# A second seven-block product pair in six attention heads, with the softmax's row copies and scaling on ScalarE

## The chip, the core and the metric

The kernel runs on one core of a Trainium2 chip. The metric is the device time of one execution in microseconds (us). The engines are named as the profile names them: PE (TensorE; PEld its weight loads), DVE (VectorE), ACT (ScalarE), POOL (GpSimd) and SP (SyncE, which here issues most DMAs).

## The reference

A trunk of two pre-norm residual layers over 512 tokens of width 1024: layer 0 mixes with dilated attention, layer 1 with a Mamba-2 scan, each is followed by a gated ConvFFN, and a last RMSNorm ends it. The change lies in the attention of layer 0, which has three groups (dilations 1, 4 and 16) of eight heads of width 128:

```python
def dilated_attention_mixer(h, w_qkv, w_o, cos, sin):
    qkv = (h @ w_qkv).reshape(bsz, s, N_ATTN_GROUPS, 3, ATTN_HEADS_PER_GROUP, ATTN_HEAD_DIM)
    q = apply_partial_rope(qkv[:, :, :, 0], cos, sin)
    k = apply_partial_rope(qkv[:, :, :, 1], cos, sin)
    v = qkv[:, :, :, 2].astype(jnp.float32)
    for g in range(N_ATTN_GROUPS):
        dil = ATTN_DILATIONS[g]
        o_g, lse_g = dilated_window_attention(q[:, :, g], k[:, :, g], v[:, :, g], dil,
                                              ATTN_WINDOWS[g] // dil)
        outs.append(o_g)
        lses.append(lse_g)
    wts = jax.nn.softmax(jnp.stack(lses, axis=2), axis=2)
    o = jnp.einsum("bsgh,bsghe->bshe", wts, jnp.stack(outs, axis=2))
    return o.reshape(bsz, s, ATTN_OUT_WIDTH).astype(h.dtype) @ w_o
```

Rope turns the first 32 of a head's 128 channels. Each group has its own softmax, and the three are merged by the softmax of their log sums.

## The kernel before

**Products.** An fp32 product is made of three matmuls: every operand is split into a high part (a cast to fp32r, on ACT, L127 or L328) and a low part (operand minus high part, on DVE, L128 or L331), and `mm3` issues high by high, high by low and low by high (`long_product`, L136). A plain product of one weight unit (1024 rows in eight steps, 128 columns, all 512 tokens) is 24 matmuls of 512 columns.

**Product pairs.** The query and the key of one group and head may be made together as a `Pair`: the two 128-column outputs, halved by tokens, and the halved input form a product of 2x2 blocks that is made with seven block products in place of eight. A block is 12 matmuls of 256 columns, so a pair is 84 of these in place of 48 of 512. It loads four pieces of weights (a, b, c and q; q's tile has two buffers), makes four sums of them on DVE (`sums`, L317, L318, L320, L321), splits the four results a, b, c, d (`split`), runs the blocks 0 to 6 (`block`; 0 and 1 use a, 2 and 3 use b, 4 and 5 use c, 6 uses d), and combines their PSUM banks: `query` (DVE, L525, L527), `key` (DVE, L532 to L534), with the rope's swap of rows (`swap`, a shuffle on DVE, L541, and a product on POOL, L542) and `turn` (DVE L547, POOL L548). ACT copies block 0's and 1's banks to a kept tile (L518) and block 4's bank out (L520). `QK_PAIRS` lists the pairs: group 1 of heads 0 to 6. All other queries and keys are plain products, read by `qk_read` (DVE L465, shuffle L468, POOL L469 and L470). Of v, group 0 is made per head (`v0_step`: product, scaled copy tv on DVE, L555; then `v0_turn` transposes it on PE to pv, L562); the values of groups 1 and 2 are made in two halves for all heads, the second of them in the stage of head 4 (`late_values`).

**A head's attention.** `attend(h)` is a generator, and each `next(core)` runs one step: scores of the first two and the last two blocks of 128 queries (PE L640 to L642 for groups 0, 1, 2; DVE masks and takes the row maximum, L646, L650; ACT takes the exponentials, L652), `spread` (17 small copies that bring a row's maxima and sums from other partitions, L659, L662), `join` (the merge of the groups, DVE L668 to L676, with an exponential on ACT, L671), `weigh` (rows times their share, L683), transposes of the rows (`by_key`, PE L690, ACT L692) and values (PE L698, L703; ACT L731, DVE L732).

**What sets the order.** The projections of head h+1 are woven into the attention of head h: `attend_and_project` for h = 0 to 5, `attend_and_fetch` for h = 6. A stage is called here after the head whose projections it makes, so "the stage of head 2" is `attend_and_project(1)`. Inside `tc.manual_schedule` PE, DVE and ACT run in the order in which the code stands; SP's and POOL's orders are the scheduler's. The stage of head 2 goes from 130.70 to 175.80 us in the profile. PSUM has three banks for products, three auxiliary ones and two for scores; raw weights have four buffers and split weights five.

Of the kernel before, what the change touches and what calls it, by code (L numbers as in the profile page):

```python
# [29 lines left out]
EPS = 1e-5  # L30
NEG = -1e30
FF_PARTS = ((0, 8), (8, 8), (16, 6))
QK_PAIRS = ((0, 1), (1, 1), (2, 1), (3, 1), (4, 1), (5, 1), (6, 1))
STORED = 6


# [17 lines left out]
def trunk(ctx: ExitStack, tc: tile.TileContext, A, out):  # L54
# [48 lines left out]
    rbc = cp.tile([P, S], F32, tag="rbc", name="rbc")  # L103

    cp.tile([P, 8], F32, tag="gap", name="gap")
    k2.tile([P, 24], F32, tag="gap2", name="gap2", bufs=1)
    nc.scalar.dma_start(par[:, :C_FFN], A["par"][:, :C_FFN])
    V.memset(ones, 1.0)
    V.memset(mhalf, -0.5)
# [280 lines left out]
    for k, xp in enumerate(xps):  # L390
        square(k, xp, ssum, V)
    load2, second = v_steps(2, 0)
    minus = sm.tile([P, KD], F32, tag="minus", name="minus", bufs=1)
    V.tensor_scalar(minus, par[:, C_MIX : C_MIX + KD], -1.0, None, op0=ALU.mult)
    combined = []

# [169 lines left out]
    def qk_steps(h):  # L566
        return [
            lambda cut=None, g=g, c=c: qk_step(h, g, c, cut) for g in range(NG) for c in range(2)
        ] + [lambda: v0_step(h)]

    E = mybir.EngineType
    WRITTEN = {E.PE, E.DVE, E.Activation}

    with tc.manual_schedule(engines=WRITTEN):
        load2(1)
        V.tensor_tensor(cr, cr, rbc, op=ALU.mult)
        second[0]()
        combine(1)
        load2(2)
        V.tensor_tensor(sr[0:ROPE, :], sr[0:ROPE, :], rbc[0:ROPE, :], op=ALU.mult)  # L580
        second[1]()
        combine(2)
        load2(3)
        second[2]()
        combine(3)
        ready(0, 0, 0)
        one = Pair(0, 1)
        second[3]()
        one.sums()
        one.split("ab")  # L590
        p = qk_products(0, 0, 0)
        qk_read(0, 0, 0, p)
        one.split("cd")
        ready(0, 2, 0)
        for i in range(3):
            one.block(i)
        one.query(0)
        for i in range(3, 6):
            one.block(i)
        one.query(1)  # L600
        ready(0, 2, 1)
        one.block(6)
        one.turn(0)
        one.key()
        p = qk_products(0, 2, 0)
        ready(0, 0, 1)
        qk_read(0, 2, 0, p)
        p = qk_products(0, 2, 1)
        ready_v0(0)
        qk_read(0, 2, 1, p)  # L610
        p = qk_products(0, 0, 1)
        qk_read(0, 0, 1, p)
        ready(1, 0, 0)
        v0_step(0)
        ready(1, 0, 1)

    scale = HD ** -0.5
    oh, ol = [], []
# [1 line left out]
    def attend(h):  # L620
# [14 lines left out]
        def scores(i0):  # L635
            for i in (i0, i0 + 1):
                sc = side_bank("sc")
                ii = slice(i * P, (i + 1) * P)
                k0 = P if i == 0 else 0
                T.matmul(sc[:, k0:256], q[0][:, ii], kk[0][:, i * P - P + k0 : (i + 1) * P], start=True, stop=True)  # L640
                T.matmul(sc[:, 256:384], q[1][:, ii], kk[1][:, ii], start=True, stop=True)
                T.matmul(sc[:, 384:512], q[2][:, ii], kk[2][:, ii], start=True, stop=True)  # L642
                pr = t2("pr", "pr", 7, s3)
                prs[i] = pr
                for w, cs in enumerate((slice(k0, 256), slice(256, 512))):
                    V.tensor_tensor_reduce(  # L646
                        out=pr[:, cs], in0=sc[:, cs], in1=mask[:, cs], scale=1.0, scalar=NEG * 2,
                        op0=ALU.add, op1=ALU.max, accum_out=own[:, w, 0, i : i + 1],
                    )
                V.tensor_scalar(neg[:, :, i], own[:, 0:2, 0, i], -scale, None, op0=ALU.mult)  # L650
                for w, cs in enumerate((slice(k0, 256), slice(256, 512))):
                    SC.activation(  # L652
                        pr[:, cs], pr[:, cs], AF.Exp, bias=neg[:, w, i : i + 1], scale=scale,
                        accum_out=own[:, w, 1, i : i + 1],
                    )

        def spread():

            V.tensor_copy(own[:, 2], own[:, 0])  # L659
            for a in range(4):  # L660
                for b in range(4):
                    V.tensor_copy(oth[32 * b : 32 * b + 32, :, :, a], own[32 * a : 32 * a + 32, 1:3, :, b])  # L662

        def join():

# [13 lines left out]
        def weigh(i):  # L679
            k0 = P if i == 0 else 0  # L680
            pr = prs[i]
            for w, cs in enumerate((slice(k0, 256), slice(256, 512))):
                V.tensor_scalar(pr[:, cs], pr[:, cs], share[:, w, i : i + 1], None, op0=ALU.mult)  # L683

        def by_key(i):
            k0 = P if i == 0 else 0
# [20 lines left out]

        scores(0)
        yield
        scores(2)  # L710
        yield
        spread()
        yield
# [63 lines left out]

    def together(core):

        for n in (1, 1, 2, 2, 1, 1):  # L780
            for _ in range(n):
                next(core, None)
            yield

    def attend_and_project(h, after=()):

        core, m = attend(h), h + 1
        follow = lambda c: ready(m + 1, 0, c)
        with tc.manual_schedule(engines=WRITTEN):
            pair = Pair(m, 1)  # L790
            next(core)
            pair.sums((0,))
            v0_turn(h)
            pair.split("a")
            pair.sums((1,))
            p = qk_products(m, 0, 0)
            qk_read(m, 0, 0, p)
            pair.split("bc")
            ready(m, 2, 0)
            p = qk_products(m, 0, 1)  # L800
            qk_read(m, 0, 1, p)
            next(core)
            for i in range(3):
                pair.block(i)
            pair.query(0)
            pair.split("d")
            ready(m, 2, 1)
            for i in range(3, 5):
                pair.block(i)
            next(core)  # L810
            pair.block(5)
            pair.query(1)
            next(core)
            next(core)
            pair.block(6)
            ready_v0(m)
            pair.turn(0)
            pair.key()
            p = qk_products(m, 2, 0)
            qk_read(m, 2, 0, p)  # L820

            p = qk_products(m, 2, 1, cut=(5, lambda: next(core)))
            next(core)
            qk_read(m, 2, 1, p)
            for f in after[:2] or (lambda: follow(0), lambda: follow(1)):
                f()
            v0_step(m)
            next(core, None)
# [3 lines left out]
    def late_values():  # L832

        (l1, s1), (l2, s2) = v_steps(1, 1), v_steps(2, 1)
        loads = [lambda l=l, u=u: l(u) for l in (l1, l2) for u in range(4)]
        loads += [lambda c=c: ready(5, 0, c) for c in range(2)]
        steps = s1 + s2
        out = loads[:2]
        for i, f in enumerate(steps):
            if i + 2 < len(loads):  # L840
                out.append(loads[i + 2])
            out.append(f)
        return out

    def attend_and_fetch(h):

# [8 lines left out]

        with tc.manual_schedule(engines=WRITTEN):
            next(core)
            v0_turn(h)
            ready(m, 1, 0)
            products(0, 0)  # L860
# [2 lines left out]
            products(0, 1)  # L863
            ready(m, 1, 1)
            read(0, 1)
            next(core)
            products(1, 0)
            ready(m, 2, 0)
# [6 lines left out]
            read(1, 1)  # L875
            products(2, 0, cut=(5, lambda: next(core)))
            next(core)
            fetch_heads(1)
            read(2, 0)
            products(2, 1)  # L880
            fetch_heads(2)
            read(2, 1)
            next(core, None)

    for h in range(NH):
# [892 lines left out]
```

## Time and profile before

| | |
|---|---|
| time, median of 3 runs | 1611.13 us (1610.71 to 1611.44) |
| the profiled execution | 1610.11 us, of which its span 1608.0 us |
| busy share of the span | PE 99%, PEld 87%, DVE 77%, ACT 45%, POOL 35% |
| attention of layer 0 | about 48 to 470 us of the span |

The span goes from the first instruction to the last; the execution's own time is 2.1 us longer. Rows of a timeline give start, duration (both us), engine, line of the kernel, operation, output <- inputs with buffer numbers left out, shapes, a count where like instructions are put together, and in brackets how long the engine had stood idle and what ended that. POOL's steps have their duration from being started to being done, so that a step that stands by while another instruction goes on shows a long duration.

### The profile page before, as it was taken

The page shows a single profiled execution, that of the slowest core. Times are in us where ns is not written, and L with a number is a line of the kernel's source. Part 1 is how long each engine was busy: PE and PEld are TensorE (multiplying, and loading weights), DVE is VectorE, ACT ScalarE, POOL GpSimd, SP SyncE. Part 2 cuts the span into 40 slices and gives each one's busy share as a digit, 9 for nine tenths or more (in the row PEclk, how much of TensorE's full clock was granted, in tenths as well). Part 3 has the DMA queues.
Part 4 walks back from the last instruction along what each step waited for, and adds up shares of the span by engine and source line. Part 5 has one row for each costly group of instructions (what it writes and reads, how often), then busy time and mean ns, then how long its engine had stood idle before and what let it go on. Part 6 is the DMA issues. An engine that isn't in the chain of part 4 may idle for free.

```text
span 1608.0 us, 23435 instructions
## 1 busy us (share of the span) xinstructions
PE 1598.8 (99%) x8864; PEld 1398.7 (87%) x8864; DVE 1230.4 (77%) x2083; ACT 720.1 (45%) x1132; POOL 570.6 (35%) x432
## 2 busy tenths in 40 slices
PE   9999999999999999999999999999999999999998
PEld 8889988899888889889888888888888888988987
DVE  7788886388757868778757899978898687867864
ACT  6434332333435543544445455544443454444443
POOL 0434453045412753652331222222112285365230
PEclk9999999999999999999999999999999999999999
DMA  6322323123334323423333433323332322332341
GB/s 222 105 93 92 99 86 118 54 72 105 123 107 131 102 69 92 151 64 101 128 99 109 149 108 115 104 98 123 121 128 74 109 73 81 110 125 73 96 127 53
DMA packets 61600, 168.44 MB, mean 105 GB/s; under 512 B 7152, under 2 KB 10608, under 8 KB 61488
## 3 DMA queue, kind: packets, MB, share of 16 engines
q1 hardware_dynamic: 60928, 166.42, 32.1%
q8 instruction: 70, 1.15, 0.3%
q10 hardware_dynamic: 560, 0.53, 0.1%
q14 instruction: 42, 0.34, 0.1%
HBM read 163.19 MB, written 3.74 MB: 104 GB/s over the span
## 4 chain that ended last, share of the span: by engine, by line
PE 85%; DVE 4%; POOL 1%; issue 1%; ACT 0%; DVEq 0%; POOLq 0%; ACTq 0%
PE u L136 29%; PE qk L136 7%; PE xs L136 5%; PE wso L136 5%; PE z L136 5%; PE v L136 4%; PE b L136 3%; PE c L136 3%; PE wo L136 3%; PE wd L136 2%; PE wz L136 2%; PE py L1351 1%; PE pf L1359 1%; PE pst L1306 1%; PE qk41r L136 1%
## 5 line engine op out<-in xcount | busy, mean ns | idle before, releaser
L136 PE MATMUL u<-xh,hi_u 128*128 128x512 f32 x704 | 269.8, 383 | 0.0
L136 PE MATMUL u<-xh,lo_u 128*128 128x512 f32 x704 | 269.4, 383 | 0.0
L136 PE MATMUL u<-xl,hi_u 128*128 128x512 f32 x704 | 267.3, 380 | 0.0
L136 PEld LDWEIGHTS u<-xh,lo_u 128*128 128x128 f32 x704 | 131.7, 187 | 25.1
L128 DVE TENSOR_TENSOR lo_u<-raw_u,hi_u 128x1024 fp32r<-128x1024 f32 x88 | 123.6, 1414 | 38.9 <-ACT hi_u L127 38.9
L136 PEld LDWEIGHTS u<-xl,hi_u 128*128 128x128 f32 x704 | 131.7, 187 | 24.6
L136 PEld LDWEIGHTS u<-xh,hi_u 128*128 128x128 f32 x704 | 131.7, 187 | 22.4 <-issue 0.4
L127 ACT CAST hi_u<-raw_u 128x1024 fp32r<-128x1024 f32 x88 | 91.8, 1047 | 107.5 <-PE u L136 62.3
L469 POOL TENSOR_TENSOR rotqk<-rotqk,sr 32x512 f32<-32x512 f32 x34 | 74.4, 2188 | 157.6 <-DVE rotqk L468 157.6
L920 DVE SCALAR_TENSOR_TENSOR au<-u,par,au 128x511 f32<-128x511 f32 (+1 forms) x152 | 113.3, 746 | 20.4 <-ACT au L918 18.0
L945 POOL TENSOR_TENSOR au<-au,au 128x512 f32<-128x512 f32 x43 | 58.0, 1349 | 170.7 <-DVE au L920 156.9
L136 PE MATMUL qk<-xh,hi_qk 128*128 128x512 f32 x272 | 105.5, 388 | 0.0
L136 PE MATMUL qk<-xh,lo_qk 128*128 128x512 f32 x272 | 104.2, 383 | 0.0
L1296 POOL TENSOR_TENSOR xdd<-xdt,dec 128x384 f32<-128x384 f32 x16 | 18.0, 1139 | 241.0 <-DVE xdt L1295 241.0
L933 DVE TENSOR_TENSOR u<-u,rbc 128x512 f32<-128x512 f32 x76 | 52.8, 695 | 66.2 <-PE u L136 65.9
L136 PE MATMUL qk<-xl,hi_qk 128*128 128x512 f32 x272 | 103.4, 380 | 0.0
L918 ACT ACTIVATE au<-u,par 128x512 f32<-128x512 f32 x76 | 59.1, 778 | 22.8 <-DVE u L933 21.2
L652 ACT ACTIVATE pr<-pr,neg 128x256 f32<-128x256 f32 (+1 forms) x64 | 31.1, 487 | 76.7 <-DVE neg L650 76.3
L1096 POOL TENSOR_TENSOR xr<-xr,sums 128x512 f32<-128x512 f32 x16 | 33.1, 2069 | 82.1 <-DVE sums L1094 82.1
L239 POOL TENSOR_TENSOR ssum<-ssum,sq 128x512 f32<-128x512 f32 x21 | 32.5, 1549 | 83.2 <-ACT sq L238 82.8
L136 PEld LDWEIGHTS qk<-xh,lo_qk 128*128 128x128 f32 x272 | 50.9, 187 | 9.6
L136 PEld LDWEIGHTS qk<-xl,hi_qk 128*128 128x128 f32 x272 | 51.0, 187 | 8.8
(3304 smaller groups left out, 4773.5 us busy)
## 6 DMA issues: line engine op xcount, KB each, us to landing
raw_u<-in_wup SPq DMA_DIRECT2D x88, 512.0 KB, 3.4
raw_qk<-in_wqk SPq DMA_DIRECT2D x34, 512.0 KB, 3.4
raw_xs<-in_win SPq DMA_DIRECT2D x16, 512.0 KB, 3.3
raw_z<-in_win SPq DMA_DIRECT2D x16, 512.0 KB, 3.6
lm<-rows SPq DMA_DIRECT2D x32, 256.0 KB, 5.2
raw_wso<-in_wso SPq DMA_DIRECT2D x16, 512.0 KB, 3.3
raw_v<-in_wv SPq DMA_DIRECT2D x12, 512.0 KB, 4.4
raw_wd<-in_wdn SPq DMA_DIRECT2D x16, 384.0 KB, 3.4
```

Of the source, the lines that this page charges most:

```text
L127: SC.copy(hi[:, s], raw[:, s])
L128: low.tensor_tensor(lo[:, s], raw[:, s], hi.bitcast(F32)[:, s], op=ALU.subtract)
L136: T.matmul(in_turns(dst), w, in_turns(x), start=first, stop=last, skip_group_check=skip)
L239: add.tensor_tensor(ssum, ssum, sq, op=ALU.add)
L469: G.tensor_tensor(rot[R, :], rot[R, :], sr[R, :], op=ALU.mult)
L652: SC.activation(pr[:, cs], pr[:, cs], AF.Exp, bias=neg[:, w, i : i + 1], scale=scale, accum_out=own[:, w, 1, i : i + 1],)
L918: latest["tap"] = SC.activation(dst, src, AF.Identity, bias=col(c_b), scale=col(c_w + taps - 1))
L920: V.scalar_tensor_tensor(dst[:, j:], src[:, : S - j], col(c_w + taps - 1 - j), dst[:, j:], op0=ALU.mult, op1=ALU.add,)
L933: V.tensor_tensor(dst, p, rbc, op=ALU.mult)
L945: by.tensor_tensor(ab[1], ab[0], ab[1], op=ALU.mult)
L1096: G.tensor_tensor(low3, low3, v.unsqueeze(1).to_broadcast([P, 2, 256]), op=ALU.add)
L1296: G.tensor_tensor(v4(u[:, 0:384], 3), v4(t[:, 0:384], 3), b3(dec3[:, 0:3, heads[x]], 64), op=ALU.mult)
```

## The change

Heads 1 to 6 get a second pair, for group 2. In a stage the blocks of the two pairs now come first (`one` for group 1, `two` for group 2), and group 0's two plain products and v0 last. The first pair of the next head is begun at the end of a stage (`next_pair`: sums, splits of a and b, splits of c and d), ahead of the scores of the next stage; `late_values` does that for head 5. The exponentials become a step of their own (`powers`). The copies of `spread` and the products of `weigh` go from DVE to ACT. `attend_and_fetch` reads group 2's products before it fetches stored heads. The tile `minus` gets the place of a filler tile.

```diff
-QK_PAIRS = ((0, 1), (1, 1), (2, 1), (3, 1), (4, 1), (5, 1), (6, 1))
+QK_PAIRS = ((0, 1),) + tuple((h, g) for h in range(1, 7) for g in (1, 2))
...
-    k2.tile([P, 24], F32, tag="gap2", name="gap2", bufs=1)
+    minus = k2.tile([P, 24], F32, tag="gap2", name="minus", bufs=1)[:, :KD]
...
+    begun_pair = {}
+
+    def next_pair(h):
+
+        if h == NH - 1:
+            ready(h, 0, 0)
+            yield
+            ready(h, 0, 1)
+            yield
+        else:
+            pair = begun_pair[h] = Pair(h, 1)
+            pair.sums()
+            yield
+            pair.split("ab")
+            yield
+            pair.split("cd")
+        yield
...
-        ready(1, 0, 0)
+        following = next_pair(1)
+        next(following)
+        next(following)
         v0_step(0)
-        ready(1, 0, 1)
+        next(following)
...
         def spread():
 
-            V.tensor_copy(own[:, 2], own[:, 0])
+            SC.copy(own[:, 2], own[:, 0])
             for a in range(4):
                 for b in range(4):
-                    V.tensor_copy(oth[32 * b : 32 * b + 32, :, :, a], own[32 * a : 32 * a + 32, 1:3, :, b])
+                    SC.copy(oth[32 * b : 32 * b + 32, :, :, a], own[32 * a : 32 * a + 32, 1:3, :, b])
...
-                V.tensor_scalar(pr[:, cs], pr[:, cs], share[:, w, i : i + 1], None, op0=ALU.mult)
+                SC.activation(pr[:, cs], pr[:, cs], AF.Copy, scale=share[:, w, i : i + 1])
...
     def attend_and_project(h, after=()):
 
         core, m = attend(h), h + 1
-        follow = lambda c: ready(m + 1, 0, c)
+        follow = next_pair(m + 1)
         with tc.manual_schedule(engines=WRITTEN):
-            pair = Pair(m, 1)
+            one, two = begun_pair.pop(m), Pair(m, 2)
             next(core)
-            pair.sums((0,))
+            next(core)
             v0_turn(h)
...
+            two.sums()
+            one.block(0)
+            one.block(1)
+            two.split("a")
+            one.block(2)
+            one.query(0)
+            two.split("b")
+            for i in range(3, 6):
+                one.block(i)
+            one.query(1)
+            one.block(6)
+            one.turn(0)
+            one.key()
+            next(core)
+            two.split("c")
+            two.block(0)
+            two.block(1)
+            next(core)
+            two.block(2)
+            two.query(0)
+            two.split("d")
+            ready(m, 0, 0)
+            for i in range(3, 6):
+                two.block(i)
+            two.query(1)
+            ready(m, 0, 1)
+            next(core)
+            two.turn(0)
+            next(core)
+            next(core)
+            two.block(6)
+            two.key()
             p = qk_products(m, 0, 0)
             qk_read(m, 0, 0, p)
+            ready_v0(m)
+            if not after:
+                next(follow)
+            p = qk_products(m, 0, 1, cut=(6, lambda: next(core)))
+            next(core)
             qk_read(m, 0, 1, p)
...
+            for f in after[:2] or (lambda: next(follow),) * 2:
                 f()
             v0_step(m)
             next(core, None)
...
     def attend_and_fetch(h):
...
             products(2, 0, cut=(5, lambda: next(core)))
             next(core)
+            read(2, 0)
             fetch_heads(1)
-            read(2, 0)
             products(2, 1)
+            read(2, 1)
             fetch_heads(2)
-            read(2, 1)
```

The lines of the changed kernel are other ones: its scores' reductions are L665 and L669, the pair's steps L524 to L546, the plain readings L464 and L467, tv L554, `spread` L683 and L686, `weigh` L707. In the rows below a name has the head, the group and 0 for a query or 1 for a key at its end (qk201: head 2, group 0, key; v02: the values of head 2), and a buffer's number.

DVE in the stage of head 2, around the second pair of score reductions. Before:

```order
L331 TENSOR_TENSOR lob_qk21_1430<-rawb_qk21_1353,hib_qk21_1429 128x1024
L331 TENSOR_TENSOR loc_qk21_1434<-rawc_qk21_1354,hic_qk21_1433 128x1024
L128 TENSOR_TENSOR lo_qk220_1439<-raw_qk220_1437,hi_qk220_1438 128x1024
L465 TENSOR_TENSOR qk201_1468<-qk201_1443,cr_368 128x4x4x32
L468 STREAM_SHUFFLE rotqk201_1470<-qk201_1443 32x512
L646 ISA pr_1478,own_1360<-sc_1474,mask_372 128x256
```

And with the change, at the same place:

```order
L526 TENSOR_TENSOR qk210_1477<-qk210_1477,qk21r3_1473 128x256
L540 STREAM_SHUFFLE rotqk210_1564<-qk210_1477 32x512
L546 TENSOR_TENSOR qk210_1477<-qk210_1477,cr_367 128x512
L531 TENSOR_TENSOR qk211_1478<-keptqk21_1476,qk21r2_1474 128x256
L532 TENSOR_TENSOR qk211_1478<-qk211_1478,keptqk21_1476 128x256
L533 TENSOR_TENSOR qk211_1478<-qk211_1478,qk21r4_1475 128x256
L540 STREAM_SHUFFLE rotqk211_1584<-qk211_1478 32x512
L546 TENSOR_TENSOR qk211_1478<-qk211_1478,cr_367 128x512
L665 ISA pr_1593,own_1438<-sc_1589,mask_371 128x256
L669 TENSOR_SCALAR neg_1440<-own_1438 128x2
L331 TENSOR_TENSOR loc_qk22_1606<-rawc_qk22_1432,hic_qk22_1605 128x1024
L524 TENSOR_TENSOR qk220_1614<-keptqk22_1613,qk22r2_1611 128x256
```

Before, the split of c (loc) stood ahead of the reductions and well ahead of its blocks; now the first pair's combining and the reductions stand ahead of the second pair's loc.

DVE at the end of the same stage, up to tv02. Before:

```order
L468 STREAM_SHUFFLE rotqk221_1748<-qk221_1685 32x512
L128 TENSOR_TENSOR lo_qk300_1754<-raw_qk300_1752,hi_qk300_1753 128x1024
L128 TENSOR_TENSOR lo_qk301_1760<-raw_qk301_1758,hi_qk301_1759 128x1024
L555 TENSOR_TENSOR tv02_1789<-v02_1764,rbc_99 128x4x4x32
L732 TENSOR_TENSOR o1_1799<-o1_1799,po1_1723 128x4x4x32
```

And with the change:

```order
L317 TENSOR_TENSOR rawa_qk31_1810<-q_qk31_1813,rawb_qk31_1811 128x512
L318 TENSOR_TENSOR rawb_qk31_1811<-rawa_qk31_1810 128x512
L320 TENSOR_TENSOR rawc_qk31_1812<-rawc_qk31_1812,rawb_qk31_1811 128x512
L321 TENSOR_TENSOR q_qk31_1813<-rawa_qk31_1810,q_qk31_1813 128x512
L464 TENSOR_TENSOR qk201_1883<-qk201_1822,cr_367 128x4x4x32
L467 STREAM_SHUFFLE rotqk201_1885<-qk201_1822 32x512
L331 TENSOR_TENSOR loa_qk31_1890<-rawa_qk31_1810,hia_qk31_1889 128x1024
L331 TENSOR_TENSOR lob_qk31_1894<-rawb_qk31_1811,hib_qk31_1893 128x1024
L331 TENSOR_TENSOR loc_qk31_1898<-rawc_qk31_1812,hic_qk31_1897 128x1024
L331 TENSOR_TENSOR lod_qk31_1902<-q_qk31_1813,hid_qk31_1901 128x512
L554 TENSOR_TENSOR tv02_1930<-v02_1905,rbc_99 128x4x4x32
```

Two splits of plain weights in front of tv02 became four sums and four splits of head 3's pair.

ACT in the same stage, between the second exponentials and the split of v. Before:

```order
L127 CAST hi_qk221_1545<-raw_qk221_1544 128x1024
L520 COPY qk210_1499<-qk21r1_1494 128x256
L671 ACTIVATE join_1608<-join_1608 128x16
L127 CAST hi_v02_1639<-raw_v02_1638 128x1024
L692 COPY pt_1705<-pp_1701 128x384
```

And with the change:

```order
L519 COPY qk220_1614<-qk22r1_1609 128x256
L127 CAST hi_qk201_1711<-raw_qk201_1710 128x1024
L683 COPY own_1438<-own_1438 128x8
L686 COPY oth_1439<-own_1438 32x4 x16
L695 ACTIVATE join_1735<-join_1735 128x16
L707 ACTIVATE pr_1445<-pr_1445,join_1735 128x128
L707 ACTIVATE pr_1445<-pr_1445,join_1735 128x256
L707 ACTIVATE pr_1453<-pr_1453,join_1735 128x256 x2
L707 ACTIVATE pr_1593<-pr_1593,join_1735 128x256 x2
L707 ACTIVATE pr_1601<-pr_1601,join_1735 128x256 x2
L127 CAST hi_v02_1805<-raw_v02_1804 128x1024
L716 COPY pt_1845<-pp_1841 128x384
```

The 17 copies now stand behind a split and behind the copy that waits for the second pair's block 4, and the eight scalings stand ahead of the split of v and of the copies of the transposed rows.

More of the change, by code (lines that the diff above doesn't have):

```diff
@@ L392, in trunk @@
     load2, second = v_steps(2, 0)
-    minus = sm.tile([P, KD], F32, tag="minus", name="minus", bufs=1)
     V.tensor_scalar(minus, par[:, C_MIX : C_MIX + KD], -1.0, None, op0=ALU.mult)
@@ L650, in scores, with powers @@
                 V.tensor_scalar(neg[:, :, i], own[:, 0:2, 0, i], -scale, None, op0=ALU.mult)
+        def powers(i0):
+            for i in (i0, i0 + 1):
+                k0 = P if i == 0 else 0
+                pr = prs[i]
                 for w, cs in enumerate((slice(k0, 256), slice(256, 512))):
@@ L709, in attend @@
         yield
+        powers(0)
+        yield
         scores(2)
+        yield
+        powers(2)
         yield
@@ L778, in together @@
     def together(core):
-        for n in (1, 1, 2, 2, 1, 1):
+        for n in (2, 2, 2, 2, 1, 1):
             for _ in range(n):
@@ L787, in attend_and_project @@
         core, m = attend(h), h + 1
-        follow = lambda c: ready(m + 1, 0, c)
+        follow = next_pair(m + 1)
         with tc.manual_schedule(engines=WRITTEN):
-            pair = Pair(m, 1)
+            one, two = begun_pair.pop(m), Pair(m, 2)
             next(core)
-            pair.sums((0,))
+            next(core)
             v0_turn(h)
-            pair.split("a")
-            pair.sums((1,))
+            two.sums()
[30 more added lines that the diff above has]
+            two.key()
@@ L796, in attend_and_project @@
             p = qk_products(m, 0, 0)
             qk_read(m, 0, 0, p)
-            pair.split("bc")
-            ready(m, 2, 0)
-            p = qk_products(m, 0, 1)
-            qk_read(m, 0, 1, p)
[L802 to L825, printed above, removed]
+            ready_v0(m)
+            if not after:
+                next(follow)
@@ L835, in late_values @@
         loads = [lambda l=l, u=u: l(u) for l in (l1, l2) for u in range(4)]
-        loads += [lambda c=c: ready(5, 0, c) for c in range(2)]
+        follow = next_pair(5)
+        loads += [lambda: next(follow)] * 3
         steps = s1 + s2
@@ L842, in late_values @@
             out.append(f)
-        return out
+        return out + loads[len(steps) + 2 :]
     def attend_and_fetch(h):
@@ L857, in attend_and_fetch @@
             next(core)
+            next(core)
             v0_turn(h)
@@ L865, in attend_and_fetch @@
             read(0, 1)
+            next(core)
             next(core)
```

## The prediction

> **What bounds the kernel now.** The first view to read is the page: its span, the busy shares, the granted clock and the chain of work that ended last.
>
> ```profile
> span 1608.0 us, 23435 instructions
> PE 1598.8 (99%) x8864; PEld 1398.7 (87%) x8864; DVE 1230.4 (77%) x2083; ACT 720.1 (45%) x1132; POOL 570.6 (35%) x432
> PEclk9999999999999999999999999999999999999999
> PE 85%; DVE 4%; POOL 1%; issue 1%; ACT 0%; DVEq 0%; POOLq 0%; ACTq 0%
> ```
>
> PE is busy in 1598.8 of 1608.0 us at the full clock in all 40 slices, and the chain is PE's. So time is won only by taking matmuls away, and lost wherever PE is made to wait. The second view is PE's waits between 48 and 475 us, the attention, where the whole change lies; the third is the timeline of the longest of them (idle time before an instruction and its releaser stand in brackets).
>
> ```profile
> PE sc L642 <- POOL qk L470: 1.5, 3, 1.0
> 448.40 0.71 PE L642 MATMUL sc<-qk,qk 128*128 128x128 f32 x4 [1.03 <-POOL qk L470]
> ```
>
> Three waits for POOL's rope additions, 1.5 us together, are all that PE loses there. The fourth view gives busy times in stretches: one product pair in the plain form (48 matmuls), two pairs of seven blocks (84 matmuls), and a whole head of the attention. Columns are the length, then PE, PEld, DVE, ACT, POOL, the clock and the DMA.
>
> ```profile
> 132.73:143.37 10.64, 10.64 (x52) 9.06 (x50) 9.28 (x22) 6.35 (x13) 2.27 (x1) 1.00 0.25 80
> 145.04:154.88 9.84, 9.84 (x87) 9.84 (x86) 7.53 (x28) 4.56 (x13) 4.29 (x4) 1.00 0.45 142
> 99.91:109.75 9.84, 9.84 (x87) 9.84 (x86) 7.50 (x30) 4.56 (x13) 3.94 (x4) 1.00 0.47 148
> 130.70:175.80 45.10, 45.10 (x280) 40.80 (x279) 37.52 (x91) 17.13 (x35) 20.39 (x13) 1.00 0.27 85
> ```
>
> In a head PE has no gap, but DVE works 37.5 of 45.1 us: it is the engine that can come too late. ACT works 17.1.
>
> **The change, part by part.**
>
> (1) Products. Six pairs of group 2 (heads 1 to 6) go from 10.64 to 9.84 us, one block being 9.84/7 = 1.41: 6 x 0.80 = **-4.8 us**, and both pair rows say the same 9.84.
>
> (2) Old waits. A head's scores no longer end on group 2's plain products, and `attend_and_fetch` reads its last two products before the fetches: the 1.5 us have no cause left, **-1.5 us** (bounds -1.5 and 0).
>
> (3) The split of c. The second pair's block 4 needs DVE's low part of c, which now stands behind the first pair's turn and key and behind the scores' reductions. The rows of the same work in the kernel before:
>
> ```profile
> 104.45 0.42 DVE L525 TENSOR_TENSOR qk<-keptqk,qk11r 128x256 f32<-128x256 f32 x1 [1.77 <-PE qk11r L136]
> 163.20 0.41 DVE L532 TENSOR_TENSOR qk<-keptqk,qk21r 128x256 f32<-128x256 f32 x1
> 163.45 1.26 POOL L548 TENSOR_TENSOR qk<-qk,rotqk 32x512 f32<-32x512 f32 x1 [5.26 <-DVE qk L547]
> 163.65 1.35 DVE L533 TENSOR_TENSOR qk<-qk,keptqk 128x256 f32<-128x256 f32 x1
> 165.03 0.42 DVE L534 TENSOR_TENSOR qk<-qk,qk21r 128x256 f32<-128x256 f32 x1
> 165.59 0.73 DVE L541 STREAM_SHUFFLE rotqk<-qk 32x512 f32<-32x512 f32 x1
> 166.36 0.69 DVE L547 TENSOR_TENSOR qk<-qk,cr 128x512 f32<-128x512 f32 x1
> 166.97 0.68 DVE L465 TENSOR_TENSOR qk<-qk,cr 128x512 f32<-128x512 f32 x1
> 145.57 0.40 DVE L646 CUSTOM_DVE_ANT_0 pr<-sc,mask 128x256 f32<-128x256 f32 x1
> 147.62 0.54 DVE L650 TENSOR_SCALAR neg<-own 128x2 f32<-128x2 f32 x1
> 88.23 0.17 DVE L650 TENSOR_SCALAR neg<-own 128x2 f32<-128x2 f32 x1
> 143.19 1.21 DVE L128 TENSOR_TENSOR lo_qk<-raw_qk,hi_qk 128x1024 fp32r<-128x1024 f32 x1
> ```
>
> DVE starts 0.33 us after a block: the third block of the pair of 99.91 ends at 99.91 + 36 x 0.117 = 104.12, L525 starts at 104.45. Then, from start to start: query and shuffle 0.54 + 0.77, turn 0.61, key 0.45 + 1.38 + 0.54, shuffle 0.77, turn 0.61, scores 2.59 (145.57 to 148.16), split 1.2: 0.33 + 9.46 = 9.8 us after block 5 of the first pair. PE gets there after block 6 (1.41), six score matmuls (145.04 - 143.37 = 1.67), four blocks (5.62) and two matmuls (0.23): 8.9. So PE waits 0.9; where L533 is not held up by POOL (0.43, as for L534) and L650 takes 0.17 as at 88.23, DVE is there at 8.1 and PE doesn't wait. The first pair's four rope steps on POOL fall into just this stretch, so I take most of it, 0.7: 6 x 0.7 = **+4.2 us** (bounds 0 and 6 x 0.9).
>
> (4) The end of head 0. There tv (L555), which PE's transposes to pv want, used to stand behind one split:
>
> ```profile
> 81.79 1.20 DVE L128 TENSOR_TENSOR lo_qk<-raw_qk,hi_qk 128x1024 fp32r<-128x1024 f32 x1
> 85.82 0.69 DVE L555 TENSOR_TENSOR tv<-v,rbc 128x512 f32<-128x512 f32 x1 [2.83 <-PE v L136]
> 81.96 2.16 POOL L469 TENSOR_TENSOR rotqk<-rotqk,sr 32x512 f32<-32x512 f32 x1 [2.47 <-DVE rotqk L468]
> 84.20 1.27 POOL L470 TENSOR_TENSOR qk<-qk,rotqk 32x512 f32<-32x512 f32 x1
> 87.18 0.60 PE L562 MATMUL pv<-ident,tv 128*128 128x128 f32 x4
> 89.19 0.69 DVE L317 TENSOR_TENSOR rawa_qk<-q_qk,rawb_qk 128x512 f32<-128x512 f32 x1
> 89.91 0.69 DVE L318 TENSOR_TENSOR rawb_qk<-rawa_qk 128x512 f32<-128x512 f32 x1
> ```
>
> Now four sums stand there (2.66: two of 0.72, the start of L317 to that of L318, and two like a turn, 0.61) and two splits (2 x 1.14, start to start at 142.05 and 143.19), nearly all with two inputs in SBUF, and POOL's two steps come between them. Such a step costs DVE between 0.93 (what L533 lost) and 1.27 (POOL alone, 84.20); I take 1.1. 81.79 + 2.66 + 2.28 + 2.2 + 0.65 = 89.6, where pv is wanted at 87.18: **+2.4 us**. DVE's idle 2.83 us before tv are used up in this sum. Bounds: 0.3 if neither step is exposed (87.4), 3.4 if the scores, wanted at 85.6, have to wait until both steps are done after DVE.
>
> (5) The end of heads 1, 2, 3 and 5, where the next head's pair is prepared in front of tv. Before, in head 2:
>
> ```profile
> 152.65 2.81 DVE L662 COPY oth<-own 32x4 f32<-32x4 f32 x16
> 159.42 2.12 DVE L683 TENSOR_SCALAR pr<-pr,join 128x128 f32<-128x128 f32 x8
> 170.24 3.85 DVE L128 TENSOR_TENSOR lo_qk<-raw_qk,hi_qk 128x1024 fp32r<-128x1024 f32 x2
> 170.87 2.14 POOL L470 TENSOR_TENSOR qk<-qk,rotqk 32x512 f32<-32x512 f32 x1
> 174.21 0.69 DVE L555 TENSOR_TENSOR tv<-v,rbc 128x512 f32<-128x512 f32 x1
> 175.79 0.39 PE L640 MATMUL sc<-qk,qk 128*128 128x128 f32 x2
> ```
>
> Counted from the end of the pair's block 5 (154.88 - 1.41 = 153.47), tv ended at 174.9, 21.4 us later. PE wants it after block 6 (1.41), the stretch from 154.88 to 175.79 and six score matmuls (1.56 at head 0, 85.62 to 87.18): 23.9. So 2.5 us were to spare. In that stretch DVE's work changes so:
> - the copies across partitions, which ended at 155.46, no longer hold it up; it starts at 153.47 + 0.33: -1.7
> - the scaling goes: -2.1
> - the split of group 0's key comes in: +1.14
> - four sums: +2.66; four splits (3 x 1.14 + 0.61) for two: +1.75
> - one more POOL step is exposed: +1.1. [...]
> - the join waits for ACT's copies: +0.3, from (6)
>
> 21.4 + 3.15 = 24.55: 0.65 us late in each of four heads, **+2.6 us** (bounds 0, with no step more exposed, and 4 x 1.75, with two). Head 4 has late value products in front of the next scores, and head 6 prepares plain weights, so neither is counted.
>
> [...]
>
> ```profile
> 140.93 1.19 DVE L331 TENSOR_TENSOR lob_qk<-rawb_qk,hib_qk 128x1024 fp32r<-128x1024 f32 x1
> 141.10 4.43 POOL L469 TENSOR_TENSOR rotqk<-rotqk,sr 32x512 f32<-32x512 f32 x1 [9.99 <-DVE rotqk L468]
> 142.05 1.21 DVE L331 TENSOR_TENSOR loc_qk<-rawc_qk,hic_qk 128x1024 fp32r<-128x1024 f32 x1
> ```
>
> POOL's step stood for 4.43 us while DVE ran three splits back to back. [...]
>
> (6) ACT takes over 17 copies and eight scalings. Nearest rows:
>
> ```profile
> 158.25 0.22 ACT L671 ACTIVATE join<-join 128x16 f32<-128x16 f32 x1 [5.52 <-DVE join L670]
> 146.94 0.51 ACT L652 ACTIVATE pr<-pr,neg 128x256 f32<-128x256 f32 x1 [5.71 <-DVE neg L650]
> ```
>
> A copy costs up to 0.22 us, at least the 0.16 that DVE took (2.81/16): 17 make 2.8 to 3.7. A scaling costs up to 0.51: eight make 4.1. That is 8 us on 17.1 of a stage of 44, beside PE's products. Two deadlines remain. The copies stand behind the copy out of the second pair's block 4 (0.4) and a split (1.05), so they end 4.3 to 5.2 us after block 4; DVE wants them 1.41 + 0.33 + 1.3 (query, shuffle) + 1.1 + 0.6 = 4.7 after it. So the join waits 0 to 0.5, and I take 0.3. The scaled rows are wanted by the transposes 10.7 us after block 5 (1.41, a plain product of 5.32, three quarters of the next); join and the first four scalings are through at about 9.6, so 1.1 us are to spare, and a late join costs PE beyond that. Nothing is charged.
>
> (7) Weights come in the same number of bytes, in an order in which each is asked for at least as early before its use; DMA is at 0.27 in a head. At nothing.
>
> **Sum** against the profiled execution's 1610.11 us: -4.8 - 1.5 + 4.2 + 2.4 + 2.6 = +2.9, or 1613.0. The median of the runs (1611.13) stands 1.0 above that execution: **1614 us**.
>
> **The rivals.**
> - *DVE's cover holds* (the other side, faster): every late DVE result in (3) to (5) is due to POOL's steps. If these fall under instructions that read PSUM or shuffle (the scores, the readings of products, the additions from PSUM), DVE is 0.8 us early at c and on time at tv, and -6.3 + 0.3 stay: 1604 + 1 = 1605. It decides from one exposed step in (3) and from none more in (5). For it speaks that in before's head no PE wait comes from DVE at all; against it that L533, in the very stretch, was hit.
> - *Only c and head 0 are late* (no change): the tails keep 0.7 us, if the join isn't held up and no step more is exposed. -6.3 + 4.2 + 2.4 = +0.3: 1611.4. For it: 0.65 us late out of 24 is a small margin.
> - *POOL is starved* (slower): DVE keeps the pair through the last splits as at 141.10. The last two steps of POOL then start when these are over, at 24.55 - 0.65 - 2.2 = 21.7, and end at 24.2, where the first scores are wanted at 1.41 + 20.91 = 22.3; with three or four steps left 24.6. Two to 2.3 us late a head for 0.65, and 3.4 for 2.4 at head 0: 1614 + 6.6 + 1.0 = 1621. Against it: the longest wait for POOL's steps before is 1.03.
> - *The pairs aren't what they say*: the order has 84 matmuls of 256 columns in place of 48 of 512, as in the rows of 9.84. I leave it without a chance.
>
> **How the numbers follow.** Forecast 0.46; cover holds 0.26; only c and head 0 0.20; POOL starved 0.08. A measurement here tells about 0.2% from no change, so "same" is 1607.9 to 1614.4. The forecast's own range is 1611 (the tails of (5) on time) to 1619 ((5) at its upper bound, 4.4 more, and half of (4)'s); it lies across the upper edge, and 0.33 of it counts as slower and 0.13 as same, since (4) and (5) can grow by more than (5) can shrink. With the second rival's 0.17 same and 0.03 slower: faster 0.26, same 0.30, slower 0.44. The range reaches from the first rival, 1604 with some of its bound, to the last, 1622; outside are what lies beyond both ends.
>
> **What would show it.** Right: a second pair of 9.84 us in six heads; no wait of PE at L642's successor for POOL near 447 us; PE waiting 0.5 to 0.9 us for DVE at the pair's block 4 in six heads, for tv in front of pv once for 2.4 us and four times for 0.65; POOL steps of 2 us and more among the next pair's splits. Wrong: no waits of PE for DVE (first rival); waits at the first scores for POOL's last addition (last rival); waits of the transposes of pr for ACT, which would say that (6) costs something; PE waiting for a DMA, against (7).

## The result, and the profile after

| | median | range, runs |
|---|---|---|
| changed kernel | 1625.13 us | 1622.88 to 1626.05, 4 |
| kernel before, beside it | 1610.92 us | 1610.66 to 1611.44, 4 |

The ratio is 1.0089, 95% interval 1.0077 to 1.0101: the change costs 14 us. The profiled execution took 1625.19 us, 15.1 more than the one of before. The page's first lines and the chain of the changed kernel:

```profile
span 1623.4 us, 24013 instructions
PE 1599.6 (99%) x9080; PEld 1408.0 (87%) x9080; DVE 1247.5 (77%) x1949; ACT 787.7 (49%) x1362; POOL 579.7 (36%) x432
PE 87%; DVE 7%; ACT 3%; POOL 2%; issue 1%; DVEq 0%; POOLq 0%; ACTq 0%
```

PE's busy time hardly moved (1598.8 to 1599.6) and the span grew by 15.4: PE waits. In the chain the share of DVE grew from 4% to 7%, that of ACT from 0% to 3% and that of POOL from 1% to 2%. PE's waits in the attention (in total, times, the longest; the line of block 4 stands for six such, one a stage):

```profile
PE sc L659 <- POOL qk L469: 11.8, 4, 3.0
PE pv L561 <- DVE tv L554: 2.1, 1, 2.1
PE qk12r L136 <- DVE loc_qk L331: 0.4, 1, 0.4
```

All three had been foreseen as possible, but the largest is that of the rival in which POOL is starved: the first scores wait for POOL's last rope addition, 11.8 us in four heads, since DVE goes on with the splits of the next head's pair while POOL's step stands by, as at 141.10 in the kernel before. The timeline of DVE at the end of the stage of head 1 shows how it comes about:

```profile
129.57 0.73 DVE L467 STREAM_SHUFFLE rotqk<-qk 32x512 f32<-32x512 f32 x1
130.21 1.20 DVE L331 TENSOR_TENSOR loa_qk<-rawa_qk,hia_qk 128x1024 fp32r<-128x1024 f32 x1
131.34 1.21 DVE L331 TENSOR_TENSOR lob_qk<-rawb_qk,hib_qk 128x1024 fp32r<-128x1024 f32 x1
132.47 1.20 DVE L331 TENSOR_TENSOR loc_qk<-rawc_qk,hic_qk 128x1024 fp32r<-128x1024 f32 x1
133.61 1.75 DVE L331 TENSOR_TENSOR lod_qk<-q_qk,hid_qk 128x512 fp32r<-128x512 f32 x1
135.29 0.67 DVE L554 TENSOR_TENSOR tv<-v,rbc 128x512 f32<-128x512 f32 x1
```

The same stretch on POOL:

```profile
130.38 4.43 POOL L468 TENSOR_TENSOR rotqk<-rotqk,sr 32x512 f32<-32x512 f32 x1 [3.22 <-DVE rotqk L467]
134.89 1.60 POOL L469 TENSOR_TENSOR qk<-qk,rotqk 32x512 f32<-32x512 f32 x1
```

And the first scores on PE:

```profile
136.54 0.80 PE L659 MATMUL sc<-qk,qk 128*128 128x128 f32 x2 [3.04 <-POOL qk L469]
```

POOL could start at 130.38, as soon as the shuffle was through, but DVE's splits of a, b and c took 1.20, 1.21 and 1.20 us (1.21 each in e7, with no POOL step beside them), and POOL's step ended 4.43 us after its start. Of the four splits only the last was longer, 1.75 us for 0.68 in e7, where POOL is done before it. POOL's last addition ended at 136.49, and PE stood still for 3.04 us. The stretches behind such waits (length, then busy times of PE, PEld, DVE, ACT and POOL, the clock, the DMA) show a second price. The rows are the scores and the transposes to pv of head 1, those of head 2, those of head 5, and then two first pairs: that of head 1, which is undisturbed, and that of head 3, which follows the scores of head 2.

```profile
136.54:140.02 3.48, 3.48 (x16) 3.30 (x17) 1.39 (x7) 0.91 (x4) 0.00 (x0) 0.56 0.50 168
186.04:188.66 2.62, 2.62 (x17) 2.57 (x17) 1.70 (x9) 0.76 (x3) 0.00 (x0) 0.76 0.64 205
373.47:375.50 2.03, 2.03 (x17) 1.98 (x17) 1.39 (x7) 0.18 (x1) 0.00 (x0) 1.00 0.43 169
90.44:100.23 9.79, 9.79 (x88) 9.79 (x86) 9.04 (x22) 6.22 (x15) 0.00 (x0) 1.00 0.56 165
188.66:199.44 10.78, 10.78 (x86) 10.78 (x85) 6.82 (x13) 5.75 (x13) 0.00 (x0) 0.90 0.26 81
```

The granted clock falls behind three of the four waits, those of heads 1 (3.04 us), 2 (3.04) and 3 (2.84). In head 1 scores and transposes take 3.48 us at 0.56, and in head 3 it is much the same (3.43 at 0.57). In head 2 they take 2.62 at 0.76 and the pair behind them 10.78 at 0.90, where an undisturbed one takes 9.79. The undisturbed length of scores and transposes is 2.01 (experiment e2 below). So these three waits cost 1.47, 1.60 and 1.42 us more than their own length, 4.5 in all. Behind the wait of head 5, as long as the others (2.93), the clock stays at 1.00.

### The profile page after: what moved, and what is told of

Its sections match the earlier page's. It is cut to its first block, busy times and chain, and to the rows that moved or that the text cites. A ratio compares the mean times of both kernels' runs of the same rounds, so it can differ in the third digit from the quotient of the medians.

```text
span 1623.4 us, 24013 instructions
## 1 busy us (share of the span) xinstructions
PE 1599.6 (99%) x9080; PEld 1408.0 (87%) x9080; DVE 1247.5 (77%) x1949; ACT 787.7 (49%) x1362; POOL 579.7 (36%) x432
## 4 chain that ended last, share of the span: by engine, by line
PE 87%; DVE 7%; ACT 3%; POOL 2%; issue 1%; DVEq 0%; POOLq 0%; ACTq 0%
PE u L136 29%; PE v L136 6%; PE z L136 5%; PE wso L136 5%; PE xs L136 5%; PE qk L136 5%; PE b L136 3%; PE c L136 3%; PE wo L136 2%; PE wd L136 2%; PE wz L136 2%; POOL rotqk L468 1%; ACT oth L686 1%; ACT pr L707 1%; PE py L1391 1%
## 5 line engine op out<-in xcount | busy, mean ns | idle before, releaser
L136 PEld LDWEIGHTS u<-xl,hi_u 128*128 128x128 f32 x704 | 131.7, 187 | 23.9
L541 POOL TENSOR_TENSOR rotqk<-rotqk,sr 32x512 f32<-32x512 f32 x26 | 53.2, 2047 | 184.6 <-DVE rotqk L540 184.6
L468 POOL TENSOR_TENSOR rotqk<-rotqk,sr 32x512 f32<-32x512 f32 x22 | 51.2, 2327 | 71.2 <-DVE rotqk L467 71.2
L136 PE MATMUL qk<-xh,hi_qk 128*128 128x512 f32 x176 | 68.3, 388 | 0.0
L136 PE MATMUL qk<-xh,lo_qk 128*128 128x512 f32 x176 | 67.5, 384 | 0.0
L136 PE MATMUL qk<-xl,hi_qk 128*128 128x512 f32 x176 | 66.9, 380 | 0.0
L1445 POOL TENSOR_TENSOR lm<-lm,cb 128x512 f32<-128x512 f32 x32 | 47.5, 1508 | 25.5 <-ACT lm L1378 25.5
L982 ACT ACTIVATE au<-au 128x512 f32<-128x512 f32 x44 | 27.8, 631 | 54.9 <-DVE au L960 54.9
```

The lines of the kernel that those rows point to most:

```text
L136: T.matmul(in_turns(dst), w, in_turns(x), start=first, stop=last, skip_group_check=skip)
L468: G.tensor_tensor(rot[R, :], rot[R, :], sr[R, :], op=ALU.mult)
L541: G.tensor_tensor(rot[R, :], rot[R, :], sr[R, :], op=ALU.mult)
L1445: G.tensor_tensor(t, t, cb, op=ALU.mult)
```

## The experiments

Theory A: POOL is starved. In four stages the first of its last two steps stands by, for 4.43 us in the row above, while DVE runs its splits back to back; the order does the harm. Theory B: DVE has too much work in a stage, in whatever order. Apart from these: is the half clock the price of the waiting, and what do ACT's copies and scalings cost?

**e1: splits of c and d behind tv.**

```diff
-            for f in after[:2] or (lambda: next(follow),) * 2:
+            for f in after[:2] or (lambda: next(follow),):
                 f()
             v0_step(m)
+            if not after:
+                next(follow)
```

> Two of the four splits of the next head's pair (c and d) go behind tv in the stages of heads 1, 2, 3 and 5; the work is the same, only its order changes. [...] Theory B (DVE has too much work in the stage, in whatever order): the same wait moves to tv and pv or stays with POOL, 2.5 to 3 us a head: 1623 to 1626.

Measured: 1622.75 us, ratio to before 1.0078 [1.0063, 1.0093]. By theory A it should have been about 1615, an estimate: POOL 1.1 to 1.7 us earlier, the first scores waiting 1.3 to 1.9 us for 3.0, and the clock at 1.00 behind these waits, as it is behind the 2.06 us at head 0 of the changed kernel. So 1622.75 lies between the theories' numbers, and nearer to B's. The timeline of POOL at the end of the same stage:

```profile
130.22 3.29 POOL L468 TENSOR_TENSOR rotqk<-rotqk,sr 32x512 f32<-32x512 f32 x1 [3.22 <-DVE rotqk L467]
133.58 2.12 POOL L469 TENSOR_TENSOR qk<-qk,rotqk 32x512 f32<-32x512 f32 x1
```

DVE's split of c there:

```profile
132.90 1.69 DVE L331 TENSOR_TENSOR loc_qk<-rawc_qk,hic_qk 128x1024 fp32r<-128x1024 f32 x1
```

And the first scores on PE:

```profile
135.75 0.51 PE L659 MATMUL sc<-qk,qk 128*128 128x128 f32 x2 [2.32 <-POOL qk L469]
```

POOL is 1.3 us earlier with its first step (133.51 for 134.81), as by A; its second then takes 0.85 us more than the 1.27 that one takes alone, beside the split of c, which neither said. A wait of 2.3 to 2.4 us a head is left. Behind these waits the clock falls in heads 1 and 5 and stays at 1.00 in heads 2 and 3; scores and transposes of head 1 (at 0.55) and of head 3:

```profile
135.75:139.33 3.58, 3.58 (x16) 3.40 (x17) 2.69 (x10) 0.98 (x4) 0.00 (x0) 0.55 0.70 242
232.29:234.30 2.01, 2.01 (x17) 1.96 (x17) 2.01 (x6) 0.00 (x0) 0.00 (x0) 1.00 0.83 256
```

Two splits in front are enough to make POOL late; e1 alone doesn't decide between A and B.

**e2: the wait filled.** Thirteen matmuls whose result nobody reads stand ahead of the first scores in heads 1, 2, 3 and 5.

```diff
+            if h in (1, 2, 3, 5):
+                fill = mm_bank(f"fill{h}")
+                for i in range(13):
+                    T.matmul(in_turns(fill), xh[0][:, 0:P], in_turns(xh[1]), start=True, stop=True)
             next(core)
```

> Thirteen matmuls of 512 columns (2.9 us) into a bank that nobody reads stand ahead of the first scores of heads 1, 2, 3 and 5, where PE waits for POOL in the changed kernel; nothing else changes. Theory A with the clock as its second price (PE's clock falls to half because PE stood still for some 3 us): the waits are filled, the clock stays at 1.00 through these stages, the twelve score matmuls take 1.7 us in place of 3.1, 4 x 1.4 us come back: 1619 to 1620. Rival (the scores run slowly for another reason, such as operands that POOL has only just written or cold weights): they stay slow and the time is 1625 or a little above.

Measured: 1621.49 us, ratio 1.0070 [1.0055, 1.0085], 3.6 below the changed kernel though PE does more. The scores and transposes of head 1:

```profile
136.68:138.69 2.01, 2.01 (x17) 1.96 (x17) 1.38 (x7) 0.16 (x1) 0.00 (x0) 1.00 0.68 256
```

2.01 us at 1.00 of the clock for 3.48 at 0.56, with the same operands from the same POOL step. So the half clock came from PE standing still, not from these operands. Of the 5.6 us that I expected 3.6 came back (4.0 in the profiled executions): there were only three halved clocks to undo, 4.5 us, and the fill makes the scores start a little later, 0.14 us in head 1.

**e3: spread and weigh on DVE again**, in the changed kernel.

```diff
-            SC.copy(own[:, 2], own[:, 0])
+            V.tensor_copy(own[:, 2], own[:, 0])
...
-                SC.activation(pr[:, cs], pr[:, cs], AF.Copy, scale=share[:, w, i : i + 1])
+                V.tensor_scalar(pr[:, cs], pr[:, cs], share[:, w, i : i + 1], None, op0=ALU.mult)
```

> The changed kernel with spread and weigh on DVE again. If ACT's 17 copies (3.5 us, for which DVE's join waits 0.7 us a head) are what makes DVE late, the waits get shorter: below 1620. [...]

Measured: 1655.08 us, ratio 1.0278 [1.0263, 1.0294], far above the 1620 of the other side and beyond theory A too, which from the 5 us that DVE gets back in a stage was put at 1632 to 1640, an estimate. PE's largest waits:

```profile
PE sc L659 <- POOL qk L469: 26.1, 5, 6.2
PE v L136 <- DVE lo_v L128: 4.3, 6, 0.7
PE po L722 <- DVE qk L533: 3.2, 6, 0.6
```

The scores wait up to 6.2 us, about 3 more in each of four heads, and behind the first of them the granted clock is 0.59 from 142.40 to 146.00 us (over the whole span 0.989, for 0.996 in the changed kernel); other products and the values wait too, in all six heads. With two pairs DVE has no room for these 5 us: ACT's edit doesn't cause the loss here but avoids 30 us.

**e4: ACT's edit alone**, in the kernel before (the same lines, the other way round).

> The kernel before with spread and weigh on ACT and nothing else. Both theories: PE has no wait for either there, so nothing changes beyond 1 us: 1610 to 1612. If the row copies on ACT cost something by themselves, the transposes of the rows wait for ACT: 1613 to 1618.

Measured: 1614.83 us, ratio 1.0029 [1.0017, 1.0040]. It costs 4.5 us by itself. That is a number of the second case, but the transposes of the rows wait for ACT only once, 0.8 us; the larger part comes by a way that I hadn't named. DVE in the stage of head 2:

```profile
163.33 1.23 DVE L128 TENSOR_TENSOR lo_v<-raw_v,hi_v 128x1024 fp32r<-128x1024 f32 x1 [4.20 <-ACT hi_v L127]
```

And ACT there:

```profile
159.17 3.20 ACT L683 ACTIVATE pr<-pr,join 128x128 f32<-128x128 f32 x8 [0.95 <-DVE join L676]
162.27 1.03 ACT L127 CAST hi_v<-raw_v 128x1024 fp32r<-128x1024 f32 x1
```

In the old order the cast of v's weights stands behind the eight scalings on ACT, and DVE waits 4.2 us for it, with the pair's turn and key and group 2's readings queued behind. POOL's last step is late then, and the scores wait five times, 3.4 us in all, for 1.5 in the kernel before.

**e5: the split of c early**, in the changed kernel.

```diff
+            two.split("c")
             one.query(1)
             one.block(6)
             one.turn(0)
             one.key()
             next(core)
-            two.split("c")
```

> The changed kernel with the second pair's split of c ahead of the first pair's last query step, in six stages. The wait at block 4 was 0.4 us each in the trace. If it comes from DVE's chain in front of c's low part, it is gone and 2.2 us come back, less what the later scores cost: 1622 to 1624. If DVE's lost time only moves to the end of the stage, POOL's last step is as much later as the wait was: 1625.

Measured: 1633.83 us, ratio 1.0146 [1.0132, 1.0160]. The waits at block 4 are gone, and the ones for POOL are 4.2 us for 3.0. The split delays the scores' reductions, so ACT's exponentials, so the cast of d behind them. DVE in the stage of head 1:

```profile
110.20 0.69 DVE L331 TENSOR_TENSOR lod_qk<-q_qk,hid_qk 128x512 fp32r<-128x512 f32 x1 [1.35 <-ACT hid_qk L328]
```

In the changed kernel that split starts at 108.81, and DVE's rows stay about 1.1 us later than there up to tv. DVE has no slack from the first pair's key to the end of the stage: what stands earlier there is paid at the end. It is paid more than once, since the clock is now halved in all four heads and for twice as long, here in head 1:

```profile
136.25:143.07 6.82, 5.47 (x23) 5.29 (x24) 4.57 (x15) 2.05 (x9) 1.29 (x1) 0.50 0.41 149
```

**e6: head 0's tv first.**

```diff
-        next(following)
-        next(following)
         v0_step(0)
+        next(following)
+        next(following)
         next(following)
```

> The changed kernel with head 0's v product and tv ahead of the sums and splits of head 1's pair. If tv was late because of the instructions in front of it, the one wait of 2.1 us at pv goes: 1623. If head 1's first blocks then wait for their split weights instead, it is 1624 to 1628.

Measured: 1627.60 us, ratio 1.0106 [1.0092, 1.0120]. The wait at pv is gone, and head 1's block 0 waits 2.6 us for a's low part and 0.6 for its cast, with the clock at 0.50 behind it: the second case, at its edge.

**e7: reads first.** In the four stages the sums of the next pair go behind the reading of group 0's key.

```diff
-    def next_pair(h):
+    def next_pair(h, later=False):
...
             pair = begun_pair[h] = Pair(h, 1)
+            if later:
+                yield
             pair.sums()
...
-        follow = next_pair(m + 1)
+        follow = next_pair(m + 1, later=m + 1 < NH - 1)
...
+            if not after and m + 1 < NH - 1:
+                next(follow)
             for f in after[:2] or (lambda: next(follow),) * 2:
```

> In the stages of heads 1, 2, 3 and 5 the reading of group 0's key goes ahead of the four sums of the next pair, so that POOL gets its last two steps some 3 us earlier, before the four splits run back to back. Nothing else is moved. Theory A: POOL is done by about 131.5 where the scores are wanted at 133.3, no wait for POOL is left and no fall of the clock; tv, still behind all four splits, may now be late by 0 to 2 us: 1608 to 1616. Theory B: the lost 3 us show up at tv in full, since DVE has that much too much work: 1620 to 1625.

Measured: 1612.99 us, ratio 1.0017 [1.0007, 1.0027]: 12 us come back by order alone. POOL's last two steps of the stage:

```profile
128.37 1.72 POOL L468 TENSOR_TENSOR rotqk<-rotqk,sr 32x512 f32<-32x512 f32 x1
130.17 1.61 POOL L469 TENSOR_TENSOR qk<-qk,rotqk 32x512 f32<-32x512 f32 x1
```

Of PE's waits the largest:

```profile
PE pv L561 <- DVE tv L554: 5.0, 5, 2.1
```

POOL is done at 131.8, and no wait for it is left. DVE's work is the same, and what it is late with shows at pv: 5.0 - 2.1 = 2.9 us in four heads, 0.7 each. That decides for A; B's share is those 0.7. The 12 us are 8.9 of waits (11.8 for 2.9) and 2.9 of the clock (4.5 for 1.6). The 1.6 are new: the wait at head 0 is 2.06 us as in the changed kernel, where the clock stayed at 1.00 behind it, and here it halves the clock in head 1's first pair, which takes 11.40 us for 9.79:

```profile
90.08:93.49 3.41, 3.41 (x18) 3.41 (x18) 3.31 (x14) 1.50 (x7) 0.00 (x0) 0.50 0.73 227
```

**e8 to e11: towards a version without waits.** e8 is e7 with the splits of c and d behind tv, the split of c early (e5) and head 0's tv first (e6).

> Reads first as in e7, with the splits of c and d behind tv as in e1, the split of c early as in e5 and head 0's tv first as in e6. Theory A: PE waits nowhere in the attention for more than 0.5 us, and what is left of the change is the six pairs (4.8) and the old waits (1.5): 1604 to 1607, faster than the kernel before. Theory B: waits of 2 us or more a head remain: 1615 or above.

Measured: 1615.63 us, ratio 1.0032 [1.0019, 1.0045]; B's number, but not its mechanism: no wait of 2 us a head remains. e6's waits of 2.6 and 0.6 us at head 1's block 0 came along, and the halved clock behind them. e10 leaves e5 and e6 out and takes head 0 otherwise:

```diff
+        following = next_pair(1)
+        next(following)
         p = qk_products(0, 0, 1)
         qk_read(0, 0, 1, p)
-        following = next_pair(1)
-        next(following)
         next(following)
         v0_step(0)
         next(following)
```

> Reads first (e7) with the splits of c and d behind tv in the four stages, and at head 0 the four sums of head 1's pair ahead of the reading of group 0's key, where DVE stands idle for 3.9 us in the kernel before. By theory A the time is the kernel before less 6.3 plus the waits that are left: the four at pv fall from 0.73 to about 0.25 each, the 2.1 at head 0 to 0 to 0.5, the six at block 4 stay at 0.35. That is 1610.1 - 6.3 + 1.0 + 0.3 + 2.1 = 1607. If the early sums hold up DVE at head 0 (their weights not yet loaded), 1609 to 1611.

Measured: 1607.88 us, ratio 0.9985 [0.9976, 0.9994]. The first scores wait 1.6 us at head 0 now, the waits at pv are gone, and those at block 4 have grown to 0.7 to 0.8 us in four heads. e9 is e10 with c early:

> e10 with the split of c early as in e5. There it moved all of DVE's work by 1.1 us and lost more at the stage's end than it won at block 4. If the stage's end has room now (reads first), 2.1 us of waits go and about 1 us comes back at block 6: 1606. If not, the tails pay 1.1 us in four heads for the 2.1 won: 1609.

Measured: 1611.92 us, ratio 1.0010 [1.0001, 1.0019]; the expectation's bad case, and worse: c early costs 4 us even where the stage's end has room. Of these, 1.6 lie in the first pairs of heads 2, 3, 4 and 6 (10.2 us each for 9.8); the rest isn't placed. e11 is e10 with the split of b behind tv too (`split("a")`, then `split("bcd")`):

> e10 with the split of b behind tv as well. The remaining 0.25 us at pv go in four heads, 1.0 us: 1606. If PE then waits for b's low part at block 2 of the next stage, the time is that of e10 or above: 1607 to 1609.

Measured: 1607.38 us, ratio 0.9980 [0.9972, 0.9989]. It beats both kernels. At pv there was nothing left to win; the first scores at head 0, where the split of b moved as well, wait 0.5 us for 1.6. PE's largest waits (the first two lines stand for four like them):

```profile
PE qk22r L136 <- DVE loc_qk L331: 0.8, 1, 0.8
PE qk62r L136 <- DVE loc_qk L331: 0.7, 1, 0.7
PE sc L661 <- POOL qk L469: 0.5, 1, 0.5
```

What the tails no longer cost is partly paid at block 4, where c's split is 0.7 to 0.8 us late in four heads.

**e12: only the tile `minus` moved**, in the kernel before. From the first product of the FFN on, the kernel with the whole change took 2.2 us less than the kernel before in the traces.

```diff
-    k2.tile([P, 24], F32, tag="gap2", name="gap2", bufs=1)
+    minus = k2.tile([P, 24], F32, tag="gap2", name="minus", bufs=1)[:, :KD]
...
-    minus = sm.tile([P, KD], F32, tag="minus", name="minus", bufs=1)
```

> The kernel before with only the tile minus in the place of the filler tile, which shifts what lies behind it in SBUF; no instruction more or less. In every kernel that has the change whole, the part behind the attention is 2.2 us shorter than in the kernel before (1100.8 to 1100.9 us from the first product of the FFN on, against 1103.1), also in those with one edit undone, while the kernel before with ACT's edit alone stays at 1103.0. If the place of the tiles does that, this kernel gains it without the rest: 1100.9 from that product on, and 1608.0 to 1608.8 in all. If it comes from another part of the change, it is the kernel before: 1610 to 1611.

Measured: 1608.97 us, ratio 0.9993 [0.9984, 1.0002]. From that product on it takes 1100.9 us, as expected of the tiles' place; the total is not told from no change, as what lies ahead of that product was 1.9 us longer in its profiled execution. Part of that comes with the tile: the 216 matmuls of the late values take 48.95 us for 48.35. Which tile's place matters wasn't tried.

## Why the prediction was wrong

It forecast 1614 and a range up to 1622; 1625 came. By its steps:

- (1) Right. A pair without a wait takes 9.79 us, the first pair of head 1; the second pairs take 10.4 with their wait at block 4 and 9.8 without.
- (2) Right: the three old waits are gone.
- (3) Right: PE's idle time at block 4 is 0.36 us in six heads for 0.7, but it is counted from the modelled end of the matmul before; from start to start block 4 takes 2.02 us for 1.40, so that 0.62 are lost. The addition that POOL holds up is L532 now, with 1.04 us for the 1.35 of the quoted row, and c's low part is there 9.4 us after block 5 for 9.8.
- (4) Right: 2.1 us at pv for 2.4. (Its lower bound is 0.2 by its own sum, not 0.3.)
- (5) is the step that failed. DVE's time came out as summed: tv ended 25.0 us after the second pair's block 5 (110.96 to 135.96), for 24.55. But the step asked only when tv is wanted, 23.9 us after that block, and let each POOL step in after one split, an order that no run shows at these four splits: POOL's step stood by through three of them. Nor does a run show the source of the 1.1 us for one more step exposed: before, no POOL step of the attention lies beside the scaling (64 instructions on L683). What the changed kernel shows in the stage of head 1 is DVE's instructions of 2.22 us for 1.21 (the split of v), 1.75 and 1.66 for 0.69 (L317, L318) and 1.75 for 0.68 (the split of d), all beside POOL's steps. The scores are wanted 1.6 us earlier, POOL's addition ended 0.5 us after tv, and 0.65 us a head became 3.0: 11.8 us for 2.6. The row of 4.43 us that stood beside it had it right, to the digit.
- A term was missing: the clock behind the waits. The rival in which POOL is starved priced its waits at their length, so that even it ended at 1621 (1621.6 by its sum). Behind three of the four waits the clock cost 4.5 us; e2 won back 3.6 net. It fell behind waits of 2.84 to 3.04 us there, of 2.32 in e1 (to 0.55) and of 2.06 in e7 (to 0.50), but not behind those of 2.93 (head 5) and 2.06 (head 0) in the changed kernel.
- (6) ACT's copies take 0.21 us each start to start, near the upper bound of 0.22; the join waits 0.4 us for them in head 1, for 0.3. Once the transposes wait for a scaled row, 0.2 us. That ACT's edit costs next to nothing is true in this order and not in the old one (e4).
- (7) No wait for a DMA at PE, as said. But the place of the tiles in memory won 2.2 us behind the attention, which wasn't in the sum.

The terms as measured, with the waits as the profile counts them: -5.1 (6 x 0.85) - 1.5 + 2.2 + 2.1 + 11.8 + 4.5 - 2.2 = 11.8, against 15.1 in the profiled executions. Counted from the start of one matmul to that of the next, the waits at block 4 are 3.7 us for 2.2, that at pv 2.2 for 2.1 and those of the first scores 12.5 for 11.8, which makes 14.1. The 1.0 left over isn't placed.

The first rival (DVE's cover holds) failed at the very place that it named; with the order of e11 it is nearly what one gets, 1607.4 for 1605.

## What to carry to other kernels

Where a trace shows one engine's step standing by under a run of another's instructions (POOL's 4.43 us under three splits here, for 1.27 alone), ask not only how much work the second has but what the first must still do, and when its result is wanted: giving POOL its last input before the splits won 12 us (e7). Such a row is a measured price and is to be preferred to an assumed order of turns. Look at the clock behind a wait as well: in the changed kernel three waits of PE of 2.84 to 3.04 us cost 1.42 to 1.60 us more than their length, and one of 2.93 us did not. And work moved to an engine stands in that engine's order, so look at what comes behind it there: in e4 DVE waited 4.20 us for a cast behind ACT's eight scalings.

## What was not expected of the hardware

- The half clock came in stretches of one length. In the changed kernel:

```profile
136.21:139.62 3.41, 3.08 (x12) 2.90 (x13) 1.56 (x6) 0.51 (x3) 0.28 (x1) 0.50 0.58 198
187.41:190.82 3.41, 3.41 (x18) 3.41 (x18) 2.94 (x11) 2.56 (x9) 0.00 (x0) 0.50 0.23 88
235.19:238.60 3.41, 2.97 (x12) 2.79 (x13) 1.66 (x6) 0.40 (x3) 0.39 (x1) 0.50 0.63 222
```

Each is 3.41 us long (in e5 it is 6.82 us at 0.50 behind a wait of some 4 us), and they start 51.20 and 47.78 us apart, 15 and 14 times 3.413. In the 3.41 us ahead of each of the three PE stood idle for 2.70, 2.05 and 2.40 us. Counted off in the same steps, the wait of head 5 (2.93 us) lies across two stretches, with 1.19 us in one and 1.74 in the other, and that of head 0 (2.06 us) with 0.45 and 1.61; behind both the clock stayed at 1.00. So in this profile the price of a wait depended on where it fell, and not on its length alone.

- Which of DVE and POOL stands by isn't settled: POOL's step took 4.43 us while DVE ran three splits of 128x1024 (1.20, 1.21 and 1.20 us), but in e7 POOL's steps took 1.61 to 1.77 us beside DVE's single sums of 128x512, and it was the sums that were long (L318, L320 and L321 show 1.65 to 1.77 us there, L317 ahead of them 0.66).

- Moving one small tile made the part behind the attention faster, 2.2 us of 1103 without an instruction changed, and the late values ahead of it 0.6 us slower.
